# One-hot lookup of slots' tokens and weights: bfloat16 on six columns in place of float32 on two

## The chip, the cores and the metric

The kernel runs on one core of one Trainium2 chip. The metric is the device time of one execution in microseconds (us). The core's engines are named as in the profile: PE is TensorE's matmuls, PEld its weight loads, DVE VectorE, ACT ScalarE, POOL GpSimd, SP SyncE, which issues the large DMAs. A matmul `mm(o, l, r)` has `l` as its stationary operand (the one that is loaded as weights) and streams `r`; the result lands in PSUM.

## The reference, cut to what matters

One block of a network on 512 tokens of width 1024: a modulated norm, a gated mixer (a chunked gMLP and a gated delta net), and then a mixture of 32 experts of which each token takes 4. The change is in the last part:

```python
logits = (hf @ w_router + b_router).astype(jnp.float32)
top_val, top_idx = lax.top_k(logits, TOP_K)
weights = jax.nn.softmax(top_val, axis=-1)
...
slot_tok = ....at[dest].set(tok_flat[order])   # which token sits in an expert's slot
slot_w = ....at[dest].set(w_flat[order])       # and with what weight
...
def expert_block(args):
    tok, wt, e = args
    xb = h_pad[tok]
    gu = xb @ w_gu[e] + b_gu[e]
    gate = jnp.minimum(gu[:, :D_FF], SWIGLU_LIMIT)
    up = jnp.clip(gu[:, D_FF:], -SWIGLU_LIMIT, SWIGLU_LIMIT)
    act = gate * jax.nn.sigmoid(SWIGLU_ALPHA * gate) * (up + 1)
    return (act @ w_down[e] + b_down[e]) * wt[:, None]
```

Then the slots' rows are added up by token, and a last norm follows.

## The kernel before, in words

The mixer takes the first quarter of the time. From about 367 us on the experts run, one "place" after the other, sorted by how many tokens they have. The place's number p runs from 0 to 31, and `CAPS` gives each a fixed number of slots: 32, 64 or 96 (float32 matmuls, in units of 64 or 32 slots), or 128, 160 or 192 ("wide": the first 128 slots are done in three float32r passes on weights that ACT and DVE split into two parts, `split_w`; the rest is a second part with a unit of its own). In the order of the places the slots are 96, 32, 64, 128, 64, 192, 32, 96, 64, 128, 64, 96, 64, 160, 32, 96, 64, 128, 64, 96, 32, 160, 64, 96, 64, 128, 64, 96, 64, 128, 64, 64. So the even places from 2 on have 32 or 64 slots, and of the odd ones place 1 has 32, six have 96 (7, 11, 15, 19, 23, 27), eight are wide (3, 5, 9, 13, 17, 21, 25, 29) and place 31 has 64. Slots beyond the fixed number are done by `past`, in branches on the counts at the end.

An expert's weights come in 12 chunks of 1 MB, 8 for gate and up and 4 for down, into a ring of 14 buffers. SP issues a chunk's DMA (L1038, L1041) when the buffer is free again.

`run(p, side, between, behind)` sets by hand, for every engine, the order of a place: for each of 8 chunks k the gate and up matmuls and then `side(k)`; then the units' `act` (`swiglu`, two ACT and three DVE operations on lines 1423 to 1427); then `between()`; then `turn`, which transposes the activations on PE (L1483, in wide places L1538) and copies them out by ACT (L1485, L1540); then the 8 steps of the down matmuls with `behind(f)`.

What the change touches is found two places ahead. `hots(p + 2)` writes on DVE a one-hot table `pm` (128 tokens of a quarter by up to 128 slots, four quarters, L1283). `find(p + 2)` multiplies it on PE with `tw`, which has for each token its number (less 1000) and its weight for this expert: four accumulating matmuls for each part of a place. `numbered` copies the result from PSUM to `info` (L1294) and makes indices (L1296, L1446). `gather` fetches the rows by an indirect DMA (L1302).

Where `find(p + 2)` stands depends on p. For even p it is in `side`, behind the second chunk of gate and up matmuls. For odd p the place ahead has at most 64 slots, so `late(p)` is true and it stands in `between`, behind the transposes for the next place and before the units' own `turn`. Place 0 does the finds of 0, 1 and 2 in its own steps (`places_steps`). In all that is 35 parts, and so 140 matmuls: 3 parts in place 0, 1 in place 1, 14 in even places, 8 in the six places with 96 slots (two of them look for a place with two parts) and 9 in the wide ones.

`tw` is filled in two steps: the numbers by a copy on DVE (L1625), and the weights by `reorder` (L1631 to L1638), whose last copy from PSUM writes them into `tw`.

Of the kernel before, what the change touches and what calls it, by code (L numbers as in the profile page):

```python
# [6 lines left out]
F32 = mybir.dt.float32  # L7
F32R = mybir.dt.float32r
BF16 = mybir.dt.bfloat16
# [3 lines left out]
OP = mybir.AluOpType  # L13
AX = mybir.AxisListType
# [3 lines left out]
P = 128  # L18
# [3 lines left out]
NT = SEQ // P  # L22
NE = 32
# [22 lines left out]
N_HOTS = 2  # L46
# [3 lines left out]
OFF = 1000.0  # L50
# [6 lines left out]
def hybrid_block(tc, x, c, w_ada, b_ada, norm1_w, w_in, gm_vnorm_w, gm_w_spatial, gm_b_spatial,  # L57
# [3 lines left out]
    V, S, G, T = nc.vector, nc.scalar, nc.gpsimd, nc.tensor  # L61
# [8 lines left out]
    def mm(o, l, r, start=True, stop=True):  # L70
        T.matmul(o, l, r, start=start, stop=stop, skip_group_check=True)  # L71

    def bank(shape=None):
        return psB.tile(shape or [P, 512], F32, name="bank", tag="bank")
# [134 lines left out]
    for kk in range(2):  # L209
        for t in range(NT):  # L210
            ps = bank([P, 4, P])
# [651 lines left out]
    xp = top.enter_context(tc.tile_pool(name="xp", bufs=1, side="left", reuse_waits="tile"))  # L863
# [36 lines left out]
    wr2 = xp.tile([P, KC, NE], F32, name="wr2", tag="wr2")  # L900
# [41 lines left out]
    for ch in range(N_CHUNK):  # L942
# [5 lines left out]
        for hb, hp in pairs:  # L948
            mm(pv[rows[hb], hp, :], xfv[rows[hb], ch * 2 + hp, :], vtk[rows[hb], ch * 2 + hp, :],
               start=hp == 0, stop=ch == 0)  # L950
# [9 lines left out]
        if ch < N_CHUNK - 1:  # L960
            for hb in range(2):
                ps = bank([P, 2, P])
# [46 lines left out]
    lg = xp.tile([P, NT, NE], F32, name="lg")  # L1009
    chosen = xp.tile([P, NT, NE], F32, name="chosen")  # L1010
    top1 = xp.tile([P, NT], F32, name="top1")
    numbers = xp.tile([P, NT], F32, name="numbers")
# [16 lines left out]
    mx = moe_sb.enter_context(tc.tile_pool(name="mx", bufs=1, side="left", reuse_waits="tile"))  # L1029
# [26 lines left out]
    op = ExitStack()  # L1056
# [159 lines left out]
        lg_mm(last, half)  # L1216

    n_first = CAPS[RANKS[0]]
    first_pm = mx.tile([P, NT, P], F32, name="pm", bufs=N_HOTS)
    first_rows = [bank([P, 4, n_first]) for _ in both]  # L1220

    def first_hots(t):
# [39 lines left out]
    class Part:  # L1262
# [11 lines left out]
        def hots(self, pos):  # L1274

            first = self.first
            if (first, self.n) not in RUNS and self.n < 96:
                pos = mx.tile([P, NT, 1], F32, name="pc")
                V.tensor_scalar(pos[:, :, 0], posn[:, :, self.place.p], float(-first), None, op0=OP.add)
                first = 0  # L1280
            run = iotas[:, RUNS[first, self.n if self.m == P else P], 0:self.m]
            self.pm = mx.tile([P, NT, P], F32, name="pm", bufs=N_HOTS)[:, :, 0:self.m]
            V.tensor_tensor(self.pm, run[:, None, :].to_broadcast([P, NT, self.m]), pos.to_broadcast([P, NT, self.m]),  # L1283
                            op=OP.is_equal)

        def find(self, ps, src):
            for t in range(NT):
                mm(ps[0:self.m], self.pm[:, t, :], src(t), start=t == 0, stop=t == NT - 1)

        def numbered(self, ps, c=2):  # L1290

            m = self.m
            info = mx.tile([P, 2], F32, name="info", bufs=8, tag=self.tag("info"))
            V.tensor_copy(info[0:m, 0:c], ps[0:m])  # L1294
            idx = mx.tile([P, 1], I32, name="idx", bufs=8, tag=self.tag("idx"))
            V.tensor_scalar(idx[0:self.n], info[0:self.n, 0:1], OFF, None, op0=OP.add)  # L1296
            self.info, self.from_ = info, idx
            if len(self.units) == 1:
                self.units[0].numbered(info, idx)
# [6 lines left out]
        def spread(self):  # L1306

            if len(self.units) == 1:
                return
            ps = psT2.tile([P, 512], F32, name="t")  # L1310
            for i, u in enumerate(self.units):
                rs = slice(u.off, u.off + u.n)
                mm(ps[:, 2 * i:2 * i + 2], lanes[u.n][rs, :], self.info[rs, :])
            for i, u in enumerate(self.units):
                info = mx.tile([P, 2], F32, name="info", bufs=8, tag=self.tag("info"))
                V.tensor_copy(info, ps[:, 2 * i:2 * i + 2])
                u.numbered(info)
# [37 lines left out]
    class Place:  # L1355
# [20 lines left out]
            for part in self.parts:  # L1376
                part.hots(pos)

        def find(self, src=None, c=2):
            ps = (psT2.tile([P, 512], F32, name="t") if src is None else bank())[:, 0:4]  # L1380
            src = src or (lambda t: tw[:, t, self.p, :])
            for i, part in enumerate(self.parts):
                part.find(ps[:, 2 * i:2 * i + c], src)
            for i, part in enumerate(self.parts):
                part.numbered(ps[:, 2 * i:2 * i + c], c)

        def gather(self):
            for part in self.parts:
# [214 lines left out]
    psT2 = moe.enter_context(tc.tile_pool(name="psT2", bufs=2, space=PSUM))  # L1603
# [17 lines left out]
                V.tensor_copy(g[rs, :], g2f[rs, b * w:b * w + w])  # L1621


    tw = xp.tile([P, NT, NE, 2], F32, name="tw", tag="wr2")
    V.tensor_copy(tw[:, :, :, 0], numbers[:, :, None].to_broadcast([P, NT, NE]))  # L1625

    def reorder(src, dst):

        pt = psT2.tile([P, 4, P], F32, name="t")[0:NE]
        for t in range(NT):  # L1630
            T.transpose(pt[:, t, :], src[:, t, :], ident)  # L1631
        turned = mp.tile([P, 4, P], F32, name="post", tag="yo", bufs=1)[0:NE]
        S.activation(turned, pt, AF.Copy)
        yield
        o = psT2.tile([P, 512], F32, name="t")
        for t in range(NT):
            mm(o[:, t * 32:t * 32 + 32], turned[:, t, :], o_pm)
        V.tensor_copy(dst, o[:, 0:128].rearrange("p (t e) -> p t e", t=NT))  # L1638

    def weights():  # L1640

        V.tensor_tensor(lg, lg, top1[:, :, None].to_broadcast([P, NT, NE]), op=OP.subtract)
        S.activation(lg, lg, AF.Exp)
        V.tensor_tensor(lg, lg, chosen, op=OP.mult)
        V.tensor_reduce(top1, lg, axis=AX.X, op=OP.add)
        V.reciprocal(top1, top1)
        V.tensor_tensor(lg, lg, top1[:, :, None].to_broadcast([P, NT, NE]), op=OP.mult)
# [13 lines left out]
    def places_steps():  # L1661

        yield from reorder(posm, posn)
        yield
        hots(0)
        hots(1)
        weights()
        yield
        yield from reorder(lg, tw[:, :, :, 1])
        find(0)  # L1670
        yield
        spread(0)
        find(1)
        place[1].gather()
        yield
        spread(1)
        hots(2)
        yield
        find(2)
# [61 lines left out]
    def run(p, side, between, behind):  # L1741
# [42 lines left out]
        for u in units:  # L1784
            (last_rows if p == NE - 1 else outputs if p == NE - 2 else add_rows)(u)

    steps = places_steps()
    def side_0(k):
        next(steps, None)
# [141 lines left out]
```

## Time and profile before

| | |
|---|---|
| median of 3 runs | 1506.29 us (1496.96 to 1507.96) |
| profiled execution | 1501.39 us, of which the span of its instructions is 1499.5 us |
| PE busy in the span | 1382.1 us (92%) |
| DVE busy | 698.5 us (47%) |
| ACT busy | 472.4 us (32%) |
| granted TensorE clock, mean | 0.962 of full speed |
| matmul records of the lookup | 280 (two for each of the 140 float32 matmuls) |

The span runs from the first to the last instruction that the profiler records; 1.9 us of the execution lie around it. A busy PE says little by itself, since matmuls are pipelined: what counts is when the next one starts.

### The profile page before, as it was taken

The page shows a single profiled execution, that of the slowest core. Times are in us where ns is not written, and L with a number is a line of the kernel's source. Part 1 is how long each engine was busy: PE and PEld are TensorE (multiplying, and loading weights), DVE is VectorE, ACT ScalarE, POOL GpSimd, SP SyncE. Part 2 cuts the span into 40 slices and gives each one's busy share as a digit, 9 for nine tenths or more (in the row PEclk, how much of TensorE's full clock was granted, in tenths as well). Part 3 has the DMA queues.
Part 4 walks back from the last instruction along what each step waited for, and adds up shares of the span by engine and source line. Part 5 has one row for each costly group of instructions (what it writes and reads, how often), then busy time and mean ns, then how long its engine had stood idle before and what let it go on. Part 6 is the DMA issues. An engine that isn't in the chain of part 4 may idle for free.

```text
span 1499.5 us, 23209 instructions
## 1 busy us (share of the span) xinstructions
PE 1382.1 (92%) x9067; PEld 733.3 (49%) x9067; DVE 698.5 (47%) x1347; ACT 472.4 (32%) x728; POOL 228.2 (15%) x213
## 2 busy tenths in 40 slices
PE   5898999998899999999999999999999999999994
PEld 3555798677336554236423542562354236423731
DVE  4574538985227455118313731561274128313824
ACT  4243332322116353117112511440252116212601
POOL 2232433450010100110011011100100110001000
PEclk9999999999999999999999999999999999999997
DMA  9576431248799995999999879999997999999892
GB/s 323 168 240 205 123 114 49 73 149 347 285 387 409 398 414 215 381 405 408 391 407 407 322 287 407 396 395 406 407 407 279 407 407 404 350 406 383 314 379 112
DMA packets 113008, 478.58 MB, mean 319 GB/s; under 512 B 14725, under 2 KB 28306, under 8 KB 80122
## 3 DMA queue, kind: packets, MB, share of 16 engines
q1 hardware_dynamic: 98176, 454.10, 77.2%
q0 software_dynamic: 9568, 18.37, 5.0%
q10 hardware_dynamic: 5146, 4.54, 1.0%
q8 instruction: 73, 1.20, 0.3%
q14 instruction: 45, 0.37, 0.1%
HBM read 465.42 MB, written 17.17 MB: 322 GB/s over the span
## 4 chain that ended last, share of the span: by engine, by line
PE 77%; DVE 14%; DMA 5%; issue 2%; ACT 2%; DVEq 0%; ACTq 0%; SPq 0%
PE gu L71 59%; PE bank L71 14%; DMA ring<-in_w_gu_dram 3%; PE t L71 2%; DMA ring<-in_w_down_dram 1%; DVE f L1426 1%; DVE f L1425 1%; DVE f L1427 1%; PE gu L1483 1%; DVE wlo L1411 1%; ACT at L1485 1%; DVE rs L88 1%; DVE hlo L248 1%; DVE rs L86 0%; DMA adaw<-in_w_ada_dram 0%
## 5 line engine op out<-in xcount | busy, mean ns | idle before, releaser
L71 PE MATMUL gu<-ring,h 128*64 128x512 f32 (+1 forms) x1984 | 374.0, 599 | 0.0
L1411 DVE TENSOR_TENSOR wlo<-ring,whi 128x1024 fp32r<-128x1024 f32 x192 | 228.9, 1222 | 41.2 <-ACT whi L1410 40.9
L71 PE MATMUL gu<-ring,at 128*32 128x256 f32 (+1 forms) x1504 | 228.9, 506 | 13.4 <-ACT at L1485 13.4
L1410 ACT ACTIVATE whi<-ring 128x1024 fp32r<-128x1024 f32 x192 | 200.2, 1060 | 103.9 <-PE gu L71 78.9
L71 PEld LDWEIGHTS gu<-ring,h 128*64 128x64 f32 (+1 forms) x1984 | 101.9, 126 | 240.8 <-issue 231.9
L1423 ACT ACTIVATE f<-gu,sevens 128x512 f32<-128x512 f32 (+1 forms) x50 | 31.4, 628 | 546.2 <-PE gu L71 544.7
L1425 DVE TENSOR_SCALAR f<-gu 128x512 f32<-128x512 f32 (+1 forms) x50 | 31.0, 620 | 284.1 <-PE gu L71 261.3
L71 PEld LDWEIGHTS gu<-ring,at 128*32 128x32 f32 (+1 forms) x1504 | 63.2, 125 | 160.0 <-issue 126.4
L1302 POOL DMA_INDIRECT f<-xnd,idx x34 | 34.5, 1014 | 531.8 <-PE gu L1483 183.0
L1737 POOL DMA_INDIRECT acc<-yo,idx x30 | 53.8, 1792 | 372.7 <-DVE yo L1505 207.7
L158 POOL TENSOR_TENSOR wlo<-w,whi 128x1024 fp32r<-128x1024 f32 x32 | 79.8, 2500 | 140.9 <-ACT whi L157 117.9
L71 PE MATMUL gu<-whi,hh 128*128 128x512 f32 x256 | 83.5, 407 | 0.1
L1505 DVE SCALAR_TENSOR_TENSOR yo<-gu,info,g2x 128x512 f32<-128x512 f32 (+1 forms) x24 | 16.9, 706 | 142.7 <-PE gu L71 142.7
L71 PE MATMUL gu<-wlo,hh 128*128 128x512 f32 x256 | 81.0, 398 | 0.9 <-DVE wlo L1411 0.4
L71 PE MATMUL gu<-whi,hl 128*128 128x512 f32 x256 | 80.1, 394 | 0.0
L71 PEld LDWEIGHTS gu<-whi,hh 128*128 128x128 f32 x256 | 46.2, 188 | 28.0 <-ACT whi L1410 12.6
L71 PEld LDWEIGHTS gu<-wlo,hh 128*128 128x128 f32 x256 | 47.5, 188 | 14.7 <-DVE wlo L1411 4.2
L71 PE MATMUL bank<-hhi,whi 128*128 128x512 f32 x160 | 51.9, 446 | 1.8 <-ACT hhi L247 1.8
L71 PEld LDWEIGHTS gu<-whi,hl 128*128 128x128 f32 x256 | 48.1, 188 | 11.2
L157 ACT ACTIVATE whi<-w 128x1024 fp32r<-128x1024 f32 x32 | 33.7, 1054 | 48.2 <-PE bank L71 25.6
L71 PE MATMUL gu<-whi,ath 128*128 128x512 f32 x128 | 48.9, 466 | 0.0
L71 PE MATMUL gu<-wlo,ath 128*128 128x512 f32 x128 | 44.0, 427 | 5.0 <-DVE wlo L1411 5.0
(424 smaller groups left out, 1740.3 us busy)
## 6 DMA issues: line engine op xcount, KB each, us to landing
ring<-in_w_gu_dram SPq DMA_DIRECT2D x256, 1024.0 KB, 17.6
ring<-in_w_down_dram SPq DMA_DIRECT2D x128, 1024.0 KB, 17.3
adaw<-in_w_ada_dram SPq DMA_DIRECT2D x32, 512.0 KB, 5.2
w<-in_w_in_dram SPq DMA_DIRECT2D x24, 512.0 KB, 3.8
ada<-in_w_ada_dram SPq DMA_DIRECT2D x16, 512.0 KB, 9.8
w<-in_w_out_dram SPq DMA_DIRECT2D x8, 512.0 KB, 3.3
x<-in_x_dram SPq DMA_DIRECT2D x4, 512.0 KB
x<-in_x_dram ACTq DMA_DIRECT2D x4, 512.0 KB
```

Of the source, the lines that this page charges most:

```text
L71: T.matmul(o, l, r, start=start, stop=stop, skip_group_check=True)
L88: V.tensor_tensor(a, a, src, op=OP.mult)
L157: S.activation(hi, w, AF.Copy)
L158: G.tensor_tensor(lo, w, hi.bitcast(F32), op=OP.subtract)
L248: V.tensor_tensor(hlo[:, k, :], hT[:, k, :], hhi[:, k, :].bitcast(F32), op=OP.subtract)
L1302: G.indirect_dma_start(out=self.xg, out_offset=None, in_=xnd[:, :], in_offset=bass.IndirectOffsetOnAxis(ap=self.from_[0:self.n], axis=0), ...
L1410: S.activation(hi, w, AF.Copy)
L1411: V.tensor_tensor(lo, w, hi.bitcast(F32), op=OP.subtract)
L1423: S.activation(r, gate, AF.Relu, scale=-1.0, bias=sevens[0:n, 0:1])
L1425: V.tensor_scalar(u, up, 7.0, -7.0, op0=OP.min, op1=OP.max)
L1505: V.scalar_tensor_tensor(y, self.dn, self.wt, g2x[self.n], op0=OP.mult, op1=OP.mult)
L1737: G.indirect_dma_start(out=u.rows(acc), out_offset=bass.IndirectOffsetOnAxis(ap=u.idx, axis=0), in_=y, in_offset=None, compute_op=OP.add, ...
```

## The change

The one-hot table becomes bfloat16 (`pmb`), and the two float32 columns of `tw` become six bfloat16 columns. Columns 0 to 2 sum to the token's number less 1000: its place within a quarter, the quarter's first number less 1000, and zero. Columns 3 to 5 sum to the weight: its bfloat16 rounding, the rounding of what is left, and the rounding of what is left then. The four matmuls of a part stream six columns in place of two, and DVE sums them in threes (`tensor_reduce`) where it copied before. `reorder` now writes the weights into a float32 tile `tw_f`, and `weight_parts` makes the three columns of it: five DVE operations, once, ahead of the first find. The table of place 0's gathered rows (`first_pm`) stays float32.

```diff
-    first_pm = mx.tile([P, NT, P], F32, name="pm", bufs=N_HOTS)
+    first_pm = mx.tile([P, NT, P], F32, name="pm", bufs=1)
...
-            self.pm = mx.tile([P, NT, P], F32, name="pm", bufs=N_HOTS)[:, :, 0:self.m]
+            self.pm = mx.tile([P, NT, P], BF16, name="pmb", bufs=N_HOTS)[:, :, 0:self.m]
...
-        def find(self, ps, src):
+        def find(self, ps):
             for t in range(NT):
-                mm(ps[0:self.m], self.pm[:, t, :], src(t), start=t == 0, stop=t == NT - 1)
+                mm(ps[0:self.m], self.pm[:, t, :], tw[:, t, self.place.p, :], start=t == 0, stop=t == NT - 1)
...
-            V.tensor_copy(info[0:m, 0:c], ps[0:m])
+            V.tensor_reduce(info[0:m], ps[0:m].rearrange("p (a b) -> p a b", b=3), axis=AX.X, op=OP.add)
...
-                part.find(ps[:, 2 * i:2 * i + c], src)
+                part.find(ps[:, 6 * i:6 * i + 6])
...
-    tw = xp.tile([P, NT, NE, 2], F32, name="tw", tag="wr2")
-    V.tensor_copy(tw[:, :, :, 0], numbers[:, :, None].to_broadcast([P, NT, NE]))
+    tw = xp.tile([P, NT, NE, 6], BF16, name="tw", tag="wr2")
+    V.tensor_scalar(tw[:, :, :, 0], numbers[:, 0:1, None].to_broadcast([P, NT, NE]), OFF, None, op0=OP.add)
+    V.memset(tw[:, :, :, 2], 0.0)
+    for t in range(NT):
+        V.memset(tw[:, t, :, 1], t * P - OFF)
+    tw_f = mx.tile([P, NT, NE], F32, name="tw_f", bufs=1)
+
+    def weight_parts():
+        for i in range(3):
+            V.tensor_copy(tw[:, :, :, 3 + i], tw_f)
+            if i < 2:
+                V.tensor_tensor(tw_f, tw_f, tw[:, :, :, 3 + i], op=OP.subtract)
...
-        yield from reorder(lg, tw[:, :, :, 1])
+        yield from reorder(lg, tw_f)
+        weight_parts()
         find(0)
```

No other instruction changes its place. On DVE, between the last copy of `reorder` and the first lookup's `info`, there stands now, in place 0:

```order
L1632 CAST tw<-tw_f 128x128
L1634 TENSOR_TENSOR tw_f<-tw_f,tw 128x128
L1632 CAST tw<-tw_f 128x128
L1634 TENSOR_TENSOR tw_f<-tw_f,tw 128x128
L1632 CAST tw<-tw_f 128x128
L1294 TENSOR_REDUCE info<-t 96x2
```

Before, the `info` copy followed that of `reorder` at once. On PE, the lookup of place 0's slots stands between `reorder`'s matmuls and the next chunk's as before, with the weight load as an instruction of its own:

```order
L71 MATMUL t<-o_pm,post 128x32 x4
L71 LDWEIGHTS pmb
L71 MATMUL t<-tw,pmb 96x6
L71 LDWEIGHTS pmb
L71 MATMUL t<-tw,pmb 96x6
L71 LDWEIGHTS pmb
L71 MATMUL t<-tw,pmb 96x6
L71 LDWEIGHTS pmb
L71 MATMUL t<-tw,pmb 96x6
L71 MATMUL gu<-ring_3369,h 64x512 x4
```

Before, one row `t<-tw,pm 96x2 x4` stood in the place of these eight.

## Rows read from the trace of the kernel before

**Rows 1.** The page: span, PE's busy time, and GB/s in 40 slices.

```profile
span 1499.5 us, 23209 instructions
PE 1382.1 (92%) x9067; PEld 733.3 (49%) x9067; DVE 698.5 (47%) x1347; ACT 472.4 (32%) x728; POOL 228.2 (15%) x213
...
GB/s 323 168 240 205 123 114 49 73 149 347 285 387 409 398 414 215 381 405 408 391 407 407 322 287 407 396 395 406 407 407 279 407 407 404 350 406 383 314 379 112
```

**Rows 2.** Waits, 380 to 1480 us, PEld and SP: total us, times, longest us.

```profile
PEld gu L71 <- DMA ring<-in_w_gu_dram: 7.5, 18, 0.8
...
SPq L1038 <- PE gu L71: 279.0, 166, 4.8
```

**Rows 3.** The tile pm, the lookup's matmuls: ns min/median/max, first and last start.

```profile
L71 PE MATMUL t<-tw,pm x280: 224/251/354, 386.4 to 1406.1; 128*128 128x2 f32 x112, 128*96 128x2 f32 x28
```

**Rows 4.** Timeline of PE in place 8: start us, us, engine, line, operation.

```profile
656.98 1.05 PE L71 MATMUL t<-tw,pm 128*128 128x2 f32 x8
657.97 1.08 PE L71 MATMUL gu<-ring,h 128*64 128x512 f32 x4
```

**Rows 5.** Timeline of PE ahead of the experts: bfloat16 matmuls on 128x128 weights.

```profile
360.94 0.21 PE L71 MATMUL bank<-mb,ones_b 128*128 128x32 bf16 x2
...
361.10 0.18 PE L71 MATMUL bank<-mb,strict_b 128*128 128x32 bf16 x1
361.20 0.27 PE L71 MATMUL bank<-mb,ones_b 128*32 128x32 bf16 x4
```

**Rows 6.** Timeline of PEld, start of place 3: bfloat16 loads ahead of 512-column matmuls.

```profile
458.30 0.55 PEld L71 LDWEIGHTS <-sel_o 96*128 96x128 bf16 x4 [0.81 <-issue]
```

**Rows 7.** Timeline of place 7 (96 slots) between its gate/up and down matmuls.

```profile
637.31 0.69 DVE L1427 SCALAR_TENSOR_TENSOR f<-f 128x512 f32<-128x512 f32 x1
...
637.48 1.05 PE L71 MATMUL t<-tw,pm 128*128 128x2 f32 x8
...
638.70 0.42 DVE L1427 SCALAR_TENSOR_TENSOR f<-f 128x256 f32<-128x256 f32 x1
...
639.03 0.88 PE L1483 MATMUL gu<-ident,f 128*128 128x128 f32 x6
...
640.37 1.08 PE L71 MATMUL gu<-ring,at 128*64 128x512 f32 x4 [0.47 <-ACT at L1485]
```

**Rows 8.** Timeline of place 9 (wide), the same stretch.

```profile
703.27 0.84 PE L71 MATMUL t<-tw,pm 128*96 128x2 f32 x8
...
705.76 0.69 DVE L1427 SCALAR_TENSOR_TENSOR f<-f 128x512 f32<-128x512 f32 x1
...
706.59 0.63 PE L1538 MATMUL gu<-ident,f 128*128 128x128 f32 x4 [1.30 <-DVE info L1294]
```

**Rows 9.** Timeline of place 0: its three lookups and what follows them.

```profile
386.10 0.29 DVE L1638 COPY tw<-t 128x128 f32<-128x128 f32 x1 [6.85 <-PE t L71]
386.44 0.84 PE L71 MATMUL t<-tw,pm 128*96 128x2 f32 x8 [0.38 <-DVE tw L1638]
387.21 0.65 PE L71 MATMUL gu<-ring,h 128*64 128x512 f32 x2
...
398.50 0.16 DVE L1294 COPY info<-t 128x2 f32<-128x2 f32 x1 [5.65 <-PE t L71]
...
398.88 2.04 DVE L1621 COPY g2x<-g2f 32x256 f32<-32x256 f32 x6
```

**Rows 10.** DVE groups by line and form: busy us, mean ns of one.

```profile
L280 DVE CAST ident_b<-ident 128x128 bf16<-128x128 f32 x1 | 0.2, 220 | 0.0
```

**Rows 11.** Timeline of DVE in place 0, operations on 128 columns.

```profile
378.09 0.29 DVE L1644 TENSOR_TENSOR lg<-lg,chosen 128x128 f32<-128x128 f32 x1 [0.38 <-ACT lg L1643]
378.42 0.29 DVE L1645 TENSOR_REDUCE top<-lg 128x4 f32<-128x128 f32 x1
```

**Rows 12.** Windows at odd places' changes: stretch, us, busy times, PEclk, DMA, GB/s.

```profile
707.00:711.00 4.00, 4.00 (x14) 3.07 (x12) 3.15 (x4) 3.74 (x8) 1.01 (x1) 0.57 1.02 424
...
1201.00:1205.00 4.00, 3.53 (x28) 2.06 (x32) 1.72 (x6) 2.28 (x7) 1.08 (x1) 1.00 1.01 421
```

More of the change, by code (lines that the diff above doesn't have):

```diff
@@ L1281, in hots, with numbered @@
             run = iotas[:, RUNS[first, self.n if self.m == P else P], 0:self.m]
-            self.pm = mx.tile([P, NT, P], F32, name="pm", bufs=N_HOTS)[:, :, 0:self.m]
+            self.pm = mx.tile([P, NT, P], BF16, name="pmb", bufs=N_HOTS)[:, :, 0:self.m]
             V.tensor_tensor(self.pm, run[:, None, :].to_broadcast([P, NT, self.m]), pos.to_broadcast([P, NT, self.m]),
                             op=OP.is_equal)
-        def find(self, ps, src):
+        def find(self, ps):
             for t in range(NT):
-                mm(ps[0:self.m], self.pm[:, t, :], src(t), start=t == 0, stop=t == NT - 1)
-        def numbered(self, ps, c=2):
+                mm(ps[0:self.m], self.pm[:, t, :], tw[:, t, self.place.p, :], start=t == 0, stop=t == NT - 1)
+        def numbered(self, ps):
             m = self.m
             info = mx.tile([P, 2], F32, name="info", bufs=8, tag=self.tag("info"))
-            V.tensor_copy(info[0:m, 0:c], ps[0:m])
+            V.tensor_reduce(info[0:m], ps[0:m].rearrange("p (a b) -> p a b", b=3), axis=AX.X, op=OP.add)
             idx = mx.tile([P, 1], I32, name="idx", bufs=8, tag=self.tag("idx"))
@@ L1377, in hots, with find @@
                 part.hots(pos)
-        def find(self, src=None, c=2):
-            ps = (psT2.tile([P, 512], F32, name="t") if src is None else bank())[:, 0:4]
-            src = src or (lambda t: tw[:, t, self.p, :])
+        def find(self):
+            ps = psT2.tile([P, 512], F32, name="t")
             for i, part in enumerate(self.parts):
-                part.find(ps[:, 2 * i:2 * i + c], src)
+                part.find(ps[:, 6 * i:6 * i + 6])
             for i, part in enumerate(self.parts):
-                part.numbered(ps[:, 2 * i:2 * i + c], c)
+                part.numbered(ps[:, 6 * i:6 * i + 6])
         def gather(self):
```

## The prediction

> **What bounds the kernel now.** I read the page first. PE is busy for 92% of the span, and in most slices of the experts' stage the memory gives about 407 GB/s [rows 1]. So both PE and the DMAs could be the bound there, and the gain of a shorter matmul stage would differ. The waits tell them apart: in the 1100 us from 380 to 1480, PE waited 7.5 us for gate and up chunks, never longer than 0.8, while the DMA queue waited 279.0 us for buffers that PE had still to read, for these chunks alone [rows 2]. The ring is full or nearly so and PE empties it: PE's order is the bound, and the DMAs keep up with little to spare. The lookup stands in that order: one part takes 8 records [rows 4] of the 280 that all parts make, a quarter of a us each but overlapping [rows 3]. What it costs the path is therefore not busy time but the distance from its first matmul to the next other one: 656.98 to 657.97, 0.98 to 0.99 us [rows 4].
>
> **The change part by part.** *The price of one lookup.* Seven bfloat16 matmuls on 128x128 weights start between 360.94 and 361.10, so one in 0.027 us, and the next other matmul starts 0.10 after the last of them [rows 5]. Four lookup matmuls then take 0.08 to the start of the last and 0.10 to the next, 0.18; if the first load is no longer hidden, 0.28. I take 0.23, which saves 0.75 of the 0.98. Six columns in place of two do not show at this size. The other end: four bfloat16 loads in front of 512-column matmuls spread over 0.55 us [rows 6]; with 0.10 to the next matmul the part would cost 0.65 and save 0.33. I stay with rows 5, since they have few columns and 128 of weights, as the lookup has.
>
> [...]
>
> *Where that time is on the path.* 35 parts stand in four kinds of place.
>
> 1. The 14 in even places stand in the stream of gate and up matmuls, with PE's next matmul behind each: all of it counts. 14 x 0.75 = 10.5 us.
> 2. The 8 in places with 96 slots stand ahead of the units' transposes. There PE waits for `swiglu` on DVE. In place 7 the first unit's last operation ends at 638.00 (637.31 + 0.69), but the transposes start at 639.03 [rows 7]: PE, not DVE, is late by 1.0 us, so 0.75 comes off in full. The second unit's ends at 639.12 (638.70 + 0.42), which with the lookup shortened PE will just meet: its two transposes come last, and the down matmuls of the first unit, at 640.37, hide its copy. 8 x 0.75 = 6.0 us.
> 3. The 9 in wide places give nothing. In place 9 the lookup starts at 703.27, but the second half of the transposes starts at 706.59, and what it waited for is DVE's last `swiglu` operation, which ends at 706.45 (705.76 + 0.69) [rows 8]; it starts when the gate and up matmuls end, whatever the lookup takes. The saved time becomes idle time of PE. The same for the one in place 1.
> 4. Place 0 has three. The first has 96 columns and takes 0.77 (386.44 to 387.21) [rows 9]; it saves 0.55. The second is in the stream: 0.75. Behind the third, DVE's `info` copy waited for PE, and then come 2.04 us of copies ahead of `swiglu` [rows 9], so an earlier end moves the whole chain: 0.75. Together 2.05.
>
> *What is added.* `weight_parts` stands in place 0 between the copy at 386.10, which the first lookup waited for [rows 9], and that lookup; queued behind it on PE are the chunks of place 0. Three casts at 0.22 [rows 10] and two subtractions at 0.29, each 0.04 behind the last (378.09 + 0.29 to 378.42) [rows 11], make 0.66 + 0.58 + 0.16 = 1.4 us, all of it on the path. With the casts' columns written 12 bytes apart, a form that no row shows, they might take the subtraction's 0.29: 1.6; below, three casts at half: 1.1. The fill of the number columns comes while DVE waits for PE ahead of `reorder`'s first copy, a wait like the 6.85 us ahead of its second [rows 9], and costs nothing; without that cover it would be some 0.5 us, once. The sum in threes is bounded by 0.29, what a reduction over 128 columns takes [rows 11], against 0.16 for the copy [rows 9]: 0.13 more at most. In the stream DVE then has nothing to do but wait for PE. In wide places it stands ahead of DVE's next work, 9 x 0.13 = 1.2 us at worst; I take zero. The one-hot table is written as before; I cost it at nothing either way, since it is made on DVE well ahead of its lookup.
>
> *Sum.* 10.5 + 6.0 + 2.05 - 1.4 = 17.2 us (17.15). The profiled execution took 1501.39, so 1484.2 on its terms. It lies 4.9 below the median of the three runs and above the fastest, so I put the changed kernel's median between the two, at **1487 us**, which is 1.3% under the 1506.29.
>
> **The rivals.** *The loads cost more.* At 0.65 a part as in rows 6 the 22 parts of kinds 1 and 2 save 22 x 0.33 = 7.3, place 0 loses 0.4 (3 x 0.33 less 1.4), and the time is 1501.4 - 6.9 = 1494.5. For it: the explicit load is an instruction of its own, and the first stands behind a wait. Against: rows 5. [...]
>
> *The DMAs take PE's place as the bound.* The slices at 407 GB/s [rows 1] show no more bandwidth to be had. If the ring ran dry there, what is saved before the last such stretch would be lost again waiting for chunks. Only the last lookups, some four in even places and two with 96 slots, would then count: 6 x 0.75 = 4.5, 1496.9. Against it: PE's waits for chunks are short [rows 2], and the slices with 215, 322, 287 and 279 GB/s [rows 1] are pauses in which the ring is full, so the lead is renewed some five times; between two of them only about four lookups, 3 us, are to be made up.
>
> *The clock falls where the lookup no longer fills a gap: slower than before.* At the changes from gate and up to down in odd places PE is idle in pieces; in place 9 the granted clock was 0.57 over 4 us, in place 23 it stayed at 1.00 [rows 12]. [...] Against: in place 9, as in most wide places, the gap shows such a fall already, and in those with 96 slots the gap itself gets shorter.
>
> *More is saved.* If the ten parts of kind 3 also shortened the path, 7.5 us more: 1476.7. Against: rows 8.
>
> **How the numbers follow.** Forecast 0.68, dearer loads 0.12, DMAs 0.08, clock 0.07, more 0.05. The executions before differ among themselves by 11 us, so 4 to 5 us to either side come with every case. A range of 1475 to 1499 holds the forecast with that, most of "more", and most of the two cases at 1494 to 1497. A measurement of this kernel can tell about 1% from no change, here 15 us: the forecast's 17.2 is over that but not by much, and with its own uncertainty I give it 0.75 of its weight as faster, the rest as the same; "more" is all faster; dearer loads, DMAs and most of the clock case are the same. Faster 0.57, same 0.40, slower 0.03.
>
> **What would show it.** In the profile after, an in-stream lookup should take 0.2 to 0.3 us from its first load to the next gate and up matmul; in places with 96 slots the transposes should start about 0.7 us sooner behind the last gate and up matmul, and in wide ones not; in place 0 PE should wait some 1.4 us longer for the first lookup. PE's waits for chunks should stay short. Wrong would be: a lookup over 0.5 us; waits of PE for the ring of several us together; PEclk under 1.00 at odd places with 96 slots; or a gain in wide places.

## The result, and the profile after

The changed kernel took 1479.82 us (median of 6 runs, 1474.56 to 1480.95) against 1500.91 for the kernel before on the same chip: ratio 0.985, 95% interval 0.982 to 0.987, so 1.5% faster and clear of no change. The forecast was 1487.0, a gain of 17.2 on the profile's terms; the medians differ by 21.1 and the two profiled spans by 21.0. The range held, and the lookups gained what the sum said. But a term that was not in the sum, TensorE's granted clock, moved several us both ways: in the two traces it gained 10.7 us from place 1 on and lost 5.6 in place 0. Of the executions reported below one, with all lookups long, took 7377 us and is left out of its median.

The page of the kernel after, as in [rows 1]:

```profile
span 1478.5 us, 22919 instructions
PE 1352.2 (91%) x8927; PEld 703.1 (48%) x8927; DVE 699.8 (47%) x1357; ACT 472.2 (32%) x728; POOL 229.2 (15%) x213
```

The waits of the kernel after, 380 to 1478 us (total us, times, longest), as in [rows 2]:

```profile
PEld gu L71 <- DMA ring<-in_w_gu_dram: 11.2, 26, 0.8
SPq L1038 <- PE gu L71: 223.3, 124, 7.5
...
ACT whi L1409 <- DMA ring<-in_w_gu_dram: 4.1, 4, 1.5
```

PE has 140 matmul records less (one for each lookup matmul, where the float32 one had two). PEld waits 3.7 us more for chunks than before, ACT 4.1 in place of 0.7, and the DMA queue waits 56 us less for PE: the ring has less lead, but PE's order is still the bound.

The lookup's tile in the kernel after (ns, minimum, median, maximum, as in [rows 3]), and the timeline in place 8, as in [rows 4]:

```profile
L71 PEld LDWEIGHTS <-pmb x140: 95/96/196, 391.2 to 1382.8; 128*128 128x128 bf16 x112, 128*96 128x96 bf16 x28
L71 PE MATMUL t<-tw,pmb x140: 165/165/242, 391.2 to 1382.9; 128*128 128x6 bf16 x112, 128*96 128x6 bf16 x28
```

```profile
658.66 0.26 PE L71 MATMUL t<-tw,pmb 128*128 128x6 bf16 x4
...
658.84 1.51 PE L71 MATMUL gu<-ring,h 128*64 128x512 f32 x6
658.95 0.16 DVE L1294 TENSOR_REDUCE info<-t 128x2 f32<-128x6 f32 x1 [2.98 <-PE t L71]
```

From the lookup's first matmul to the next other one it is 0.18 us, where it was 0.98. The sum in threes takes 0.16, just what the copy took [rows 9].

Place 7 (96 slots) and place 9 (wide), timelines of the kernel after, as in [rows 7] and [rows 8]:

```profile
639.74 0.69 DVE L1426 SCALAR_TENSOR_TENSOR f<-f 128x512 f32<-128x512 f32 x1
...
639.91 0.25 PE L71 MATMUL t<-tw,pmb 128*128 128x6 bf16 x4
...
640.66 0.66 PE L1482 MATMUL gu<-ident,f 128*128 128x128 f32 x4
...
641.70 0.41 PE L1482 MATMUL gu<-ident,f 128*128 128x128 f32 x2 [0.39 <-DVE info L1294]
...
642.04 2.66 PE L71 MATMUL gu<-ring,at 128*64 128x512 f32 x16
```

```profile
704.12 0.34 PE L71 MATMUL t<-tw,pmb 128*96 128x6 bf16 x4
...
705.51 0.63 PE L1537 MATMUL gu<-ident,f 128*128 128x128 f32 x4 [1.06 <-DVE f L1426]
...
707.43 0.63 PE L1537 MATMUL gu<-ident,f 128*128 128x128 f32 x4 [1.29 <-DVE info L1294]
```

In place 7 the transposes start 0.75 behind the lookup's start, not 1.55, the last two then wait 0.39 for DVE, and that wait is hidden behind the copy of the first four. In place 9 the shorter lookup only lengthens PE's wait, from 0.56 to 1.06; the wait before was

```profile
704.67 0.63 PE L1538 MATMUL gu<-ident,f 128*128 128x128 f32 x4 [0.56 <-DVE f L1427]
```

Place 0, the timeline of the kernel after, as in [rows 9], and the window behind it (us, busy times of PE, PEld, DVE, ACT and POOL, PEclk, DMA share, GB/s):

```profile
388.85 0.29 DVE L1648 COPY tw_f<-t 128x128 f32<-128x128 f32 x1 [6.85 <-PE t L71]
389.18 0.38 DVE L1632 CAST tw<-tw_f 128x128 bf16<-128x128 f32 x1
...
391.16 0.48 PE L71 MATMUL t<-tw,pmb 128*96 128x6 bf16 x4 [2.34 <-DVE tw L1632]
```

```profile
391.00:395.00 4.00, 3.84 (x16) 1.32 (x20) 0.41 (x3) 0.00 (x0) 0.00 (x0) 0.58 0.25 98
```

From that copy to the first lookup it is now 2.31 us instead of 0.34, 1.97 more. Behind the wait the granted clock was 0.50 for 3.4 us; before, it was 1.00 from 380 to 400 us. Ahead of all this, from the start of the place on, it was 0.50 for another 5.0 us, which put the copy 2.38 us later behind that start (19.90 us instead of 17.52). And both traces have a stretch of 6.8 us at 0.50 late in place 0. Before, PE waited for `swiglu` through 2.9 us of it; in the kernel after it lies on the transposes and down matmuls (the windows of these stretches, before and after):

```profile
400.30:407.00 6.70, 3.77 (x14) 1.46 (x18) 4.21 (x10) 2.06 (x6) 0.31 (x1) 0.50 0.29 114
```

```profile
408.10:414.80 6.70, 6.31 (x26) 1.29 (x26) 0.83 (x3) 1.93 (x6) 0.00 (x0) 0.50 0.00 0
```

**The difference, place by place** (from the start of each place's gate and up matmuls to the next's, in both traces): seven of the 14 even places, where nothing else differed, gained 0.80 to 0.86 each, so with 0.80 for each of them 14 x 0.80 = 11.2; five of the six places with 96 slots gained 0.76 to 0.79 a part and the sixth, place 19, that and one fall of the clock less; 6.2 in all, without the fall; wide places 9, 13 and 29 changed by 0.03 or less. That makes 17.4. Place 0 lost 5.5: 2.0 for the weight parts, about 2.1 gained by its three lookups, and 5.6 to the clock: 2.4 at the start of the place, 1.5 behind the wait, and 1.7 in the down matmuls (15.19 us instead of 13.48), where the last stretch at half clock now falls. What is left is 9.5 us of gain from place 1 on: 10.7 from the clock, which stood at half for 27.3 us in places 1 to 30 instead of 54.6 (in place 31 for 6.8 instead of 3.4), less 1.2 for a chunk that came late (below). So the work itself gained 17.4 + 2.1 - 2.0 = 17.5, and the clock some 5 net. The last figure is that of these two traces; the timed runs agree with its direction (mean clock 0.968 and, before, 0.962 on the first chip below).

### The profile page after: what moved, and what is told of

It is laid out like the page before. It is cut to its first block, busy times and chain, and to the rows that moved or that the text cites. A ratio compares the mean times of both kernels' runs of the same rounds, so it can differ in the third digit from the quotient of the medians.

```text
span 1478.5 us, 22919 instructions
## 1 busy us (share of the span) xinstructions
PE 1352.2 (91%) x8927; PEld 703.1 (48%) x8927; DVE 699.8 (47%) x1357; ACT 472.2 (32%) x728; POOL 229.2 (15%) x213
## 4 chain that ended last, share of the span: by engine, by line
PE 78%; DVE 13%; DMA 5%; issue 2%; ACT 2%; SPq 0%; ACTq 0%; DVEq 0%
PE gu L71 59%; PE bank L71 16%; DMA ring<-in_w_gu_dram 3%; DVE f L1424 2%; DVE f L1425 2%; DVE f L1426 2%; DVE wlo L1410 1%; PE gu L1482 1%; DMA ring<-in_w_down_dram 1%; PE t L71 1%; ACT at L1484 1%; DVE rs L88 0%; DMA wsl<-in_gm_w_spatial_dram 0%; DVE hlo L248 0%; PE bank L214 0%
## 5 line engine op out<-in xcount | busy, mean ns | idle before, releaser
L71 PE MATMUL gu<-ring,h 128*64 128x512 f32 (+1 forms) x1984 | 377.8, 603 | 0.0
L71 PE MATMUL gu<-ring,at 128*32 128x256 f32 (+1 forms) x1504 | 224.7, 506 | 10.8 <-ACT at L1484 10.8
L71 PEld LDWEIGHTS gu<-ring,h 128*64 128x64 f32 (+1 forms) x1984 | 102.5, 127 | 243.7 <-issue 232.7
L71 PEld LDWEIGHTS gu<-ring,at 128*32 128x32 f32 (+1 forms) x1504 | 62.4, 125 | 154.1 <-issue 124.8
L71 PE MATMUL gu<-whi,hh 128*128 128x512 f32 x256 | 83.5, 407 | 1.3 <-ACT whi L1409 1.3
L71 PE MATMUL gu<-wlo,hh 128*128 128x512 f32 x256 | 81.0, 398 | 0.9 <-DVE wlo L1410 0.4
L71 PE MATMUL gu<-whi,hl 128*128 128x512 f32 x256 | 80.1, 394 | 0.0
L71 PEld LDWEIGHTS gu<-whi,hh 128*128 128x128 f32 x256 | 46.2, 188 | 29.1 <-ACT whi L1409 13.1
L71 PEld LDWEIGHTS gu<-wlo,hh 128*128 128x128 f32 x256 | 47.4, 188 | 14.7 <-DVE wlo L1410 4.2
L71 PEld LDWEIGHTS gu<-whi,hl 128*128 128x128 f32 x256 | 48.1, 188 | 11.2
L71 PE MATMUL bank<-hhi,whi 128*128 128x512 f32 x160 | 50.6, 435 | 1.9 <-ACT hhi L247 1.8
L71 PE MATMUL gu<-wlo,ath 128*128 128x512 f32 x128 | 43.0, 418 | 5.1 <-DVE wlo L1410 4.9
L71 PE MATMUL gu<-whi,ath 128*128 128x512 f32 x128 | 47.3, 453 | 0.0
```

## The experiments

The table has every run, four rows for each of three chips. Ratios are to the kernel before in the runs of the same chip; the clock is the mean granted clock of the timed runs. The kernel before stood at 0.962, 0.964 and 0.965 on the three chips. A "fall" below is a stretch in which the granted clock was 0.50 in place of 1.00 (half clock).

| kernel | median us | ratio to before, 95% | clock |
|---|---|---|---|
| changed kernel, again | 1479.10 | 0.983 (0.981 to 0.986) | 0.968 |
| lookups repeated, even places | 1489.96 | 0.991 (0.989 to 0.994) | 0.968 |
| lookups repeated, places with 96 slots | 1490.13 | 0.991 (0.989 to 0.993) | 0.962 |
| lookups repeated, wide places | 1471.50 | 0.982 (0.978 to 0.985) | 0.970 |
| lookups repeated, all | 1494.94 | 0.997 (0.995 to 0.999) | 0.965 |
| gaps filled | 1468.12 | 0.979 (0.976 to 0.983) | 0.978 |
| place 0's weights first | 1473.99 | 0.984 (0.980 to 0.987) | 0.970 |
| columns as planes | 1470.81 | 0.981 (0.978 to 0.984) | 0.972 |
| kernel before, again | 1499.51 | 1.000 (0.998 to 1.002) | 0.965 |
| columns as planes, again | 1477.00 | 0.986 (0.983 to 0.989) | 0.970 |
| planes, longer wait | 1483.63 | 0.990 (0.987 to 0.993) | 0.964 |
| planes, weights first, gaps filled | 1469.35 | 0.981 (0.978 to 0.984) | 0.976 |

**Where the lookup counts.** The theory was the prediction's: in even places and with 96 slots the lookup stands on the path, in wide ones not. The rivals: it counts everywhere, or the DMAs set the time. Three kernels give the lookup back about its old length in one kind of place each, without other data:

```diff
-            for t in range(NT):
-                mm(ps[0:self.m], self.pm[:, t, :], tw[:, t, self.place.p, :], start=t == 0, stop=t == NT - 1)
+            q = self.place.p
+            for t in list(range(NT)) * (8 if q in AGAIN and not self.place.own else 1):
+                mm(ps[0:self.m], self.pm[:, t, :], tw[:, t, q, :], start=t == 0, stop=t == NT - 1)
```

`AGAIN` is the list of places whose lookup is repeated.

The expectations count places by the place looked up; the lookup itself stands two places earlier. For the even places that changes nothing (they are 2 to 28). But the list 9, 13, 17, 21, 25, 29 is looked up in the six places with 96 slots, and the list with 3, 5, 7, 11 in the wide ones and in place 1. The last two of the texts here are thus each other's: what the one expects belongs to the other's kernel.

The changed kernel again: 

> The changed kernel again, as the partner of the three others on the same chip. Every theory expects the ratio measured already, about 0.985, so some 22 us less than the kernel before.

Even places: 

> The changed kernel, but in the 14 even places from 4 to 30 each lookup makes its four matmuls 8 times over, 32 in a row, which by 0.027 us from one start to the next is some 0.75 us more for a part: about what the float32 lookup cost more. Theory (in even places the lookup's whole time is on the path): 14 x 0.75 = 10.5 us slower than the changed kernel, so half of the gain gone. Rival 1 (the DMAs set the time there, the lookup does not): under 4 us. Rival 2 (the time came from elsewhere, from the clock that fell less often): anything from 0 to 20 us, with the number of stretches at half clock changed by several, each worth 1.7 us.

Places with 96 slots: 

> The changed kernel, but in the six places 9, 13, 17, 21, 25 and 29 the lookups (wide ones, by the table of places) make their four matmuls 8 times over, some 0.75 us more for each part. Theory (in wide places the lookup lies in a gap in which PE waits for swiglu on DVE): 0 to 1 us slower than the changed kernel, none of the places longer. Rival (the lookup is on the path there as well): six parts or more by 0.75, at least 4.5 us.

Wide places: 

> The changed kernel, but in the odd places 3, 5, 7, 11, 15, 19, 23, 27 and 31 the lookups make their four matmuls 8 times over, some 0.75 us more for each part; the eight parts with 96 slots stand in five of them. Theory (with 96 slots PE, not DVE, is late there, and the lookup counts): 8 x 0.75 = 6 us slower than the changed kernel, nothing from the wide parts in places 3 and 5. Rival (DVE's swiglu is as late as PE there, so that the lookup lies in its shadow): under 2 us.

The lookup in place 8 of the first, in place 7 of the second and in place 9 of the third kernel (PE's timeline; L72 and L1539 are L71 and L1537):

```profile
655.35 0.95 PE L72 MATMUL t<-tw,pmb 128*128 128x6 bf16 x32
656.24 3.22 PE L72 MATMUL gu<-ring,h 128*64 128x512 f32 x14
```

```profile
644.85 0.79 PE L72 MATMUL t<-tw,pmb 128*128 128x6 bf16 x26
...
646.13 0.88 PE L1484 MATMUL gu<-ident,f 128*128 128x128 f32 x6
647.47 4.80 PE L72 MATMUL gu<-ring,at 128*64 128x512 f32 x36 [0.47 <-ACT at L1486]
```

```profile
693.43 1.60 PE L72 MATMUL t<-tw,pmb 128*96 128x6 bf16 x32
694.89 0.63 PE L1539 MATMUL gu<-ident,f 128*128 128x128 f32 x4
...
696.75 0.52 PE L1539 MATMUL gu<-ident,f 128*128 128x128 f32 x3 [1.22 <-DVE info L1296]
```

Place by place the answer is sharp. Each of the 14 even places got longer by 0.70 in the first kernel wherever nothing else differed, the places with 96 slots by 0.66 with one part and 1.40 with two in the second, and place 9 of the third by nothing (42.94 us, 42.97 in the changed kernel), nor places 3, 5 and 17 (0.01 us or less): in place 9 the 32 matmuls, with 1.46 us longer than the float32 lookup was, fill the wait ahead of the transposes. In place 7 the wait of 0.47 ahead of the down matmuls is back, as in [rows 7].

The medians say more than that. Against the changed kernel on the same chip the first is 10.9 us slower (9.8 by places), the second 11.0 (5.4 by places), the third 7.6 faster (0 by places), though there the intervals of the ratios overlap. What the places don't explain goes with the clock in the second, 0.962, and may do so in the third, 0.970. And of two traces of the changed kernel, equal to 0.04 us in most places, seven places differ by 1.3 to 1.6 us, each with a stretch at half clock that the other trace lacks or has shorter. So even with one and the same kernel the clock can move several us from one execution to the next.

**All lookups long.** `8 if 2 < q` in the line above.

> The changed kernel, but every lookup for the places 3 to 31 makes its four matmuls 8 times over: the three kernels with repeated lookups in one. Place by place these showed 0.70 us for each of the 14 even places, 0.66 for each of the eight parts behind the places with 96 slots and nothing in the wide ones. Theory A (the gain is the lookups' time plus about 5 to 8 us that PE's clock gives back, and what gives it back is the shorter lookups): 15 us from the lookups and some 5 to 8 from the clock, so 20 to 23 slower than the changed kernel, about the time of the kernel before, with a mean granted clock near its 0.962. Theory B (what the clock gave has nothing to do with the lookups' length): 15 us, about 1494, mean clock 0.967 to 0.968 as in the changed kernel.

1494.94 us: between the two theories. Places gained and lost as in the three kernels; the clock, 0.965, was that of the kernel before on the same chip (0.964), but the ratio to it, 0.997, leaves 5.0 us of gain. Two of these are the lookup's remaining difference (0.10 in each of 22 parts). The run doesn't tell A from B.

**What the clock follows.** The rival to a fall behind idle pieces was that the falls have another reason. Matmuls of no use were put where PE waits around `swiglu`:

```diff
+    def fill(t, n, l):
+        for _ in range(n):
+            mm(t[0:l.shape[1]].rearrange("p a b -> p (a b)"), l, b3[:, 0:512], True, True)
...
```

The calls, in `turn`, are left out here.

> The changed kernel with matmuls of no use (the selection of a bias row, 512 columns in bfloat16, some 0.23 us each, into a bank that is written anew right behind them) where PE waits around swiglu: in places with one unit 3 ahead of the transposes and 2 behind them, in wide places 4 and 5 ahead of the two halves of the transposes. The idle pieces there are 0.78 to 1.06 and 0.69 and 1.29 us. Theory (the clock falls behind these idle pieces, and each fall costs up to 1.7 us): fewer stretches at half clock from place 1 to 30, mean clock 0.975 or more, 5 to 12 us faster than the changed kernel. Rival (the falls have another reason): the clock as in the changed kernel, the time the same or up to 5 us slower, where the filling is longer than the gap.

Windows from place 1 to 30, of the kernel before, the changed kernel and the one with gaps filled; then PE's timeline in place 9 of the last:

```profile
420.00:1440.00 1020.00, 972.49 (x5438) 456.79 (x5432) 423.33 (x616) 334.24 (x480) 103.13 (x76) 0.97 0.97 377
```

```profile
420.00:1425.00 1005.00, 951.94 (x5394) 432.47 (x5392) 426.39 (x622) 334.86 (x481) 104.67 (x76) 0.99 0.99 388
```

```profile
420.00:1413.00 993.00, 971.70 (x5516) 436.48 (x5515) 425.76 (x621) 334.59 (x481) 105.25 (x76) 1.00 1.00 391
```

```profile
699.22 1.02 PE L71 MATMUL gu<-b,sel_o 96*128 96x512 bf16 x4
700.33 0.66 PE L1548 MATMUL gu<-ident,f 128*128 128x128 f32 x4
700.82 1.24 PE L71 MATMUL gu<-b,sel_o 96*128 96x512 bf16 x5
702.25 0.66 PE L1548 MATMUL gu<-ident,f 128*128 128x128 f32 x4 [0.19 <-DVE f L1426]
```

With the pieces filled one fall is left between place 1 and 30, where the changed kernel's two traces had seven and eight and the kernel before 13. The clock of its six timed executions is 0.974 to 0.981, that of the changed kernel's eleven 0.964 to 0.971: the theory holds. Most falls follow PE's idle pieces around `swiglu`, though in these places none of them is longer than 1.5 us (for falls without such a piece see place 19 below). The ratio, 0.979, is some 7 us better than the changed kernel's. Part of the gain is given back to the DMAs: with DMA share 1.00 a chunk came late in place 20, which took 2.3 us longer than in the changed kernel, and PE's first split matmul of place 21 waited for it, 1.26 us in the changed kernel and 2.89 in this one:

```profile
1077.56 0.73 PE L71 MATMUL gu<-whi,hh 128*128 128x512 f32 x2 [1.26 <-ACT whi L1409]
```

```profile
1070.63 0.73 PE L71 MATMUL gu<-whi,hh 128*128 128x512 f32 x2 [2.89 <-ACT whi L1409]
```

**The weight parts in place 0.** Two edits shorten the wait for the first lookup: place 0's column alone first, or the casts writing neighbours.

```diff
-        weight_parts()
+        weight_parts(0, 1)
         find(0)
+        weight_parts(1, NE)
```

> The changed kernel, with the three weight columns made for place 0 alone ahead of the first lookup, and for the other 31 places behind it. In the changed kernel the casts and subtractions ahead of the first lookup took 2.0 us. Theory (they stand on the path there): PE waits some 1 us less for the first lookup, since five operations of a few columns still have their fixed time; the other 2 us lie beside PE's work; 1 us faster, more (another 1 to 3 us) where the clock in place 0 does not fall behind that wait. Rival (DVE is late again further on in place 0): no difference.

```diff
-    tw = xp.tile([P, NT, NE, 6], BF16, name="tw", tag="wr2")
+    tw = xp.tile([P, NT, 6, NE], BF16, name="tw", tag="wr2")
...
```

> The changed kernel with the six columns kept as planes of 32 experts, so that the casts write neighbouring bfloat16 numbers and not ones 12 bytes apart; the lookups then read their six columns 64 bytes apart. Theory (the casts took 0.38 us instead of 0.22 because of the spread writes): casts 0.22, the first lookup 0.5 us sooner behind the copy, the lookups at 0.18 us as before; in all 0.5 us faster, too little for the median to show, so the trace of place 0 decides. Rival: the casts keep 0.38, or the lookups get dearer with the spread reads, 35 parts by 0.05 or more, some 2 us slower.

DVE groups by form (busy us, mean ns of one) of the changed kernel, of the one with place 0 first and of the one with planes:

```profile
L1632 DVE CAST tw<-tw_f 128x128 bf16<-128x128 f32 x3 | 1.1, 378 | 0.1
L1634 DVE TENSOR_TENSOR tw_f<-tw_f,tw 128x128 f32<-128x128 f32 x2 | 0.7, 328 | 0.1
```

```profile
L1632 DVE CAST tw<-tw_f 128x4 bf16<-128x4 f32 x3 | 0.5, 177 | 0.1
```

```profile
L1632 DVE CAST tw<-tw_f 128x128 bf16<-128x128 f32 x3 | 0.7, 226 | 0.1
L1634 DVE TENSOR_TENSOR tw_f<-tw_f,tw 128x128 f32<-128x128 f32 x2 | 0.6, 293 | 0.1
```

PE's wait for the first lookup, 2.34 in the changed kernel, was 1.42 with place 0 first and 1.82 with the planes, as expected; lookups with six columns 64 bytes apart cost 0.01 us a place more. In both traces the fall behind that lookup was gone and place 0 took 50.3 and 49.8 us instead of 55.5; but so it was, with 50.1, in the two kernels with repeated lookups in even and in wide places, whose place 0 is the changed kernel's. And the median of the planes was 1470.81 on one chip and 1477.00 on another, ratios 0.981 and 0.986, and that of place 0 first gives 0.984: against the changed kernel's 0.983 and 0.985 no gain is shown.

**Does that wait make the fall?**

> The kernel with the six columns as planes once more, as the partner of the two others on the same chip: some 5 us faster than the changed kernel, as before, and no stretch at half clock in place 0 right behind the first lookup, for which PE waits 1.8 us.

```diff
+        for _ in range(3):
+            V.tensor_copy(tw[:, :, 5, :], tw_f)
```

> The kernel with the six columns as planes, and the last cast of the weight columns made three times more, 0.23 us each, so that PE waits 2.5 to 2.6 us for the first lookup and not 1.8. Theory (the clock falls in place 0 behind a wait as long as the changed kernel's 2.3, and not behind 1.8 or 1.4): a stretch at half clock within a few us behind the first lookup, place 0 some 5 us longer in most runs, so 3 to 6 us slower than the kernel with the planes alone. Rival (the fall there was chance): 0.8 us slower, nothing that the medians show.

The end of the longer wait in place 0, the window behind it, and the same window with the planes alone:

```profile
390.77 0.75 DVE L1636 CAST tw<-tw_f 128x128 bf16<-128x128 f32 x3
391.57 0.35 PE L71 MATMUL t<-tw,pmb 128*96 128x6 bf16 x4 [2.60 <-DVE tw L1636]
```

```profile
393.00:397.00 4.00, 4.00 (x20) 1.10 (x16) 0.00 (x0) 0.00 (x0) 0.00 (x0) 0.57 0.06 25
```

```profile
392.00:396.00 4.00, 4.00 (x28) 1.40 (x24) 1.53 (x8) 0.00 (x0) 0.00 (x0) 1.00 0.44 129
```

The kernel with the planes alone had no fall behind its wait, as expected, but was not the 5 us faster that was expected of it (0.986). With the longer wait place 0 got 2.9 us longer in the trace (52.7, 49.8) and the median 6.6, for 0.78 us more of wait; in the trace later places got longer too. But the length of the wait does not decide alone, so the theory falls as a rule: two kernels with the changed kernel's place 0 (lookups repeated in even and in wide places) had its wait and no fall behind it, and the last kernel below had the fall with a wait as short as with place 0 first. What goes with the fall in all 14 traces is when the lookup starts: 20.1 to 22.3 us behind the start of the place in the seven with it, 17.9 to 19.8 in the seven without. A longer wait makes it start later, and so does half clock at the start of the place (six of those seven; two of the others had a shorter stretch there). So the moment of the idle piece goes with the fall; that it causes it is not shown, and what sets the right moment is not settled.

**Are the falls chance?**

> The kernel before, for a second trace of it. In the first one five even places had a stretch at half clock, in seven profiles of kernels with the short lookup (repeated in some of them) none to two had. Theory (that is a property of the kernel before): again four or more of the 14 even places. Rival (chance, where the clock falls within a run differs from run to run even for one kernel): one or two.

Windows in places 10 and 19 of the kernel before, of its second trace, and of the changed kernel:

```profile
741.50:744.50 3.00, 3.00 (x10) 0.76 (x8) 0.00 (x0) 0.99 (x4) 0.00 (x0) 0.51 1.04 371
1056.00:1062.00 6.00, 5.74 (x28) 2.24 (x30) 1.22 (x7) 1.95 (x6) 2.02 (x2) 0.50 1.00 414
```

```profile
741.50:744.50 3.00, 3.00 (x10) 0.97 (x8) 0.00 (x0) 0.67 (x3) 0.00 (x0) 0.50 1.03 352
1056.00:1062.00 6.00, 5.74 (x27) 2.12 (x28) 1.23 (x7) 1.95 (x6) 2.02 (x2) 0.50 1.01 420
```

```profile
741.50:744.50 3.00, 3.00 (x16) 1.01 (x14) 0.00 (x0) 0.98 (x4) 0.00 (x0) 1.00 1.06 373
1045.50:1051.50 6.00, 5.73 (x42) 1.46 (x42) 1.32 (x8) 2.06 (x6) 2.02 (x2) 1.00 1.01 416
```

The theory holds: from place 3 on the second trace of the kernel before has its falls in the same places as the first, within 0.2 us of the same offsets, five of them in the even places 10, 12, 18, 26 and 28. So do the two traces of the planes kernel, on two chips, among themselves; the two of the changed kernel do not. Places can thus repeat, but not in every execution: the mean clock of the kernel before went from 0.958 to 0.970 in its timed runs, with 0.962 and 0.961 in these two. One fall can be tied to the lookup: place 19 (96 slots, two parts) fell in all four traces with a long lookup there (before twice, and the kernels that repeat it there) and in none of the ten others. It cost 2.7 us before (4.27 less the 1.6 of two parts). PE in place 19 of the kernel before:

```profile
1053.48 0.68 PE L1327 MATMUL t<-ident,f 32*128 32x32 f32 x8
1054.09 2.25 PE L71 MATMUL t<-tw,pm 128*128 128x2 f32 x16
1056.27 0.97 PE L71 MATMUL gu<-b,sel_o 96*64 96x512 bf16 x6
```

The clock fell at 1055.58, in the middle of the lookup, with no idle piece ahead of it. In the 14 traces seven falls from place 1 to 30 have no idle piece of 0.1 us in the 6 us ahead of them, and all seven stand in or right behind a long lookup of two parts (places 3 and 19 of both traces of the kernel before, 19 with the places with 96 slots repeated, 11 and 19 with all). So the clock does not fall behind idle pieces alone: here PE was busy, with the lookup. Why the even places fell in the kernel before is not settled: with their lookups repeated the trace has falls in two even places, 18 and 22, and the mean clock stayed at the changed kernel's 0.968.

**All that helped, together.**

> The changed kernel with all that helped: the six columns as planes, the weight columns of place 0 made first, and the matmuls of no use where PE waits around swiglu. If the parts add up (some 8 us from the filling, some 5 from place 0): 12 to 15 us faster than the changed kernel, so about 1462 to 1466, ratio to the kernel before 0.972 to 0.977, mean clock 0.98 or more. Rival (both act on the same clock and one makes the other needless): about 1468, as with the filling alone.

1469.35 us, ratio 0.981: the rival. It and the filling alone (0.979) are faster than the kernel before by about 2%. Against the changed one (0.983 and 0.985) it is 0.2 to 0.6%, with intervals that overlap. In its trace place 0 has all the changed kernel's falls, and place 20 took 3.0 us longer than there, for late chunks and a fall behind them: what is gained ahead of place 20 is in part given back.

## Why the prediction was right, and where its sum was off

*The price of one lookup* held. It was taken as 0.23 and is 0.18, so a part saves 0.80, not 0.75; the explicit loads overlap (in the stream each one's record is 0.096 us long, and the four of a part span 0.17).

*Even places*: 10.5 forecast, 11.2 measured, and given back by 9.8 when the lookups were made long. *96 slots*: 6.0 forecast, 6.2 measured, for the reason named: PE is late there, DVE is just met (0.39 us of wait) and the copy hides it. *Wide places*: nothing, as forecast; long lookups cost nothing there. *The sum in threes*: nothing, as forecast.

*Weight parts* is the mis-sized term: 2.0 us instead of 1.4, outside the bounds of 1.1 to 1.6. Casts that write 12 bytes apart took 0.38, not the 0.22 of [rows 10] nor the 0.29 that the upper end assumed, and the subtractions that read them 0.33 instead of 0.29. With the planes they were 0.23 and 0.29, and the wait for the first lookup was 0.52 us shorter.

*The clock* is the term that the sum lacked. The rival with the clock asked whether shorter work in the gaps of odd places adds falls, and gave it 7 in 100, on the slower side; a fall cost 0.9 to 1.8 us per 3.4 in the traces. That idle pieces make falls is shown by filling them (one fall left from place 1 to 30, where the changed kernel's two traces had seven and eight); that the shorter lookup adds falls in these gaps is not. In the two traces the clock worked both ways: 10.7 us of gain from place 1 on, and 5.6 lost in place 0. The net, some 5 us less 1.2 for the late chunk, is what lies between the forecast's 17.2 and the 21 measured. Place 19's 2.7 of it goes with the shorter lookup, which the prediction did not think of as a cause of falls. The loss in place 0 does not come with the edit in every execution: the two kernels with repeated lookups in even and in wide places have the same code there, no half clock at its start or behind the wait, and take 50.1 us, as before. How much of the rest the edit caused is not settled, so that the measured gain lies within 5 us of the forecast is in part luck.

*The DMAs as bound* was given 8 in 100 and showed in one place: a late chunk before place 21, 1.2 us, and 2 to 3 more in the three kernels that reached place 20 soonest (627 to 630 us behind the start of place 1, the changed kernel 634). *Dearer loads* is ruled out by the 0.18, *more in wide places* by the repeated lookups.

The median guess of 1487 moved the forecast toward the slower of the three runs shown. On the profile's own terms, 1484.2, it would have been 4 us off instead of 7.

## What to carry to other kernels

Here a group of small matmuls cost the path what lay between its first start and the start of the next other matmul (0.98 us before, 0.18 after), and only where PE was the late one (nothing in wide places): ask at each place which wait ends last, and repeat the instruction there to test it. In this kernel, bound by PE, the sum over places was good to a us (17.2 forecast, 17.5 by places), but the granted clock gave 10.7 us from place 1 on and took 5.6 in place 0; so read the time at half clock in both traces, place by place, before a remainder is given to the edit, and look at a long run of small matmuls as well as at idle pieces. Where idle pieces can't be removed, filling them with matmuls of no use is worth a try: here it gave another 0.4 to 0.6%, with intervals that overlap.

## What was not expected of the hardware

- The clock fell behind idle pieces of 0.5 to 1.5 us, often two close together, each fall 3.4 or 6.8 us long at a granted clock of 0.50 and worth 0.9 to 1.8 us per 3.4; filling them left a mean of 1.00 from 420 to 1413 us.
- It also fell without an idle piece, in or right behind 16 records of two columns or 64 matmuls of six (seven falls in 14 traces).
- 0.78 us more of wait in front of one lookup made the kernel 6.6 us slower (2.9 in that place in the trace); and two traces of the kernel before have their falls from place 3 on at the same offsets, while two of the changed kernel have not: such losses can repeat, but need not.
- A bfloat16 load of 96 columns was dearer than one of 128, both at a granted clock of 1.00: in the kernel after its records took 0.124 us in place 9, those of 128 columns 0.096 in place 8. With repeated lookups 32 lookup matmuls in a row took 0.89 us with 128 (655.35 to 656.24) and 1.46 with 96 (693.43 to 694.89), 0.028 and 0.046 each.
- A cast of 128 columns to bfloat16 took 0.38 us writing 12 bytes apart and 0.23 writing neighbours; one of 4 columns still took 0.18.
